# Foreign blocks of matmuls inside the next weight unit, five expert units per routing head, and two reordered row norms

## The chip, the cores and the metric

The kernel runs on one core of a Trainium2 chip. The metric is the device time of one execution in microseconds (us), the median of three runs. Engines are named as in the profile: PE is the matrix engine and PEld its weight loads, DVE the vector engine, ACT the scalar engine, POOL the general engine, SP the queue that issues most DMAs.

## What is computed

Two transformer-like blocks run one after the other over 16 meta tokens and 256 tokens of width 1024. The parts that the change touches, cut from the reference:

```python
# first block, after a gated convolution mixer (w_in, w_out):
q = (xf @ w_q).reshape(n_tok, 8, 256)                  # 8 routing heads
s1 = einsum("thd,hnd->thn", q[..., :128], sub_keys[:, 0]) # scores against 128 keys, twice
s2 = einsum("thd,hnd->thn", q[..., 128:], sub_keys[:, 1])
# top 16 of s1 and of s2, top 16 of their sums -> idx (of 16384 experts), gates = softmax
act = gelu(einsum("chkd,cd->chk", u[idx], xc))
out = einsum("chk,chkd->cd", act * gates, v[idx])      # 128 experts per token
# second block: rms norm, two attentions (8 heads each), sigmoid gates, then
hn = rmsnorm(h, norm_ffn_g)
h = h + (silu(hn @ w_ffn_gate) * (hn @ w_ffn_up)) @ w_ffn_down   # 2816 = 22 x 128
```

The experts are not gathered: the kernel computes all 16384 dense products with u, multiplies them by a gate matrix that is zero but for the chosen experts, and multiplies by all of v.

## The kernel before

**Units.** All weights are read as 453 units of 128x1024 numbers in one fixed list. For each unit SP loads `raw` (five buffers), ACT rounds it to `hi` and DVE computes `lo`, the rest (three buffers each). `unit()` hands out the next one and splits two ahead. A product is made of three matmuls, hi by hi, hi by lo and lo by hi.

**mm_w and mm_a.** `mm_w` makes one 128-row piece of a projection: 24 matmuls of 256 or 272 columns (eight chunks, three products) into one PSUM bank. `mm_a` accumulates a 1024-wide product over units into four banks: 12 matmuls of 512 columns per unit. The projections u (128 units of experts), q (two units per routing head), fg and fu (22 of each, the last block's gate and up projections) go through `mm_w`; v (128), wo, o and fd (22, the down projection) through `mm_a`.

**Order.** PE and SP run in the order in which the program is written. On ACT, DVE and POOL a scheduler sets the order when the program is built.

**Routing and gates.** The stage with u interleaves two other chains with the units. `route(hd)` makes the scores of a head (tile sc, four fp32 matmuls of 128 columns), then the top-16 searches on DVE. After the last head come `softmax`, `decode` and `flip`, and then `gates`, which for 64 groups of four tokens builds two one-hot factors on DVE (tiles ga, gb), multiplies them on PE (tile gp, four fp32 matmuls) and multiplies the result into the stored products on DVE and ACT (tiles ewa, ewb). A table of costs doles these chains out: after each unit `pull` runs as many of their steps as its credit allows. In the first stage a head takes two q units and `ROUTE` u units; when all heads have been started, u units go on until the chains are done, and then the rest of u runs with `gates`, until 126 units are done:

```python
    while todo:
        pull(10.0)
```

runs what is left of `gates` with no units between, then v begins with `expert_w(0)` (tiles w_hi, w_lo).

**Row norms.** In the first mixer and at the start of the second block the row scale is not applied to the input of a projection but to its result. `x_norm` (sum of squares by a matmul x_ss) and `across` (a diagonal matrix from the row scales, tile rsb_d, and two matmuls rsb_b or rsf_b) spread the scales over the partitions.

Of the kernel before, what the change touches and what calls it, by code (L numbers as in the profile page):

```python
# [1 line left out]

# [31 lines left out]
AHEAD = 400  # L34
XN = 1
SOON = 60
# [14 lines left out]
def two_blocks(ctx, tc, x, feats, vecs, w_in, w_out, w_q, keys, u, v, final_g, meta2, w_in2, lams, w_gate,  # L51
# [37 lines left out]
    units += [rows(w_out, c) for c in range(8)]  # L89
    ROUTE = 7  # L90
    nu = 0
# [70 lines left out]


    def mm_w(ps, a, cols):
        hi, lo = unit()
        ahi, alo = a
        for k in range(KC):
            ks = slice(k * P, (k + 1) * P)
            nc.tensor.matmul(ps, hi[:, ks], ahi[:, k, cols], start=(k == 0), stop=False)  # L169
            nc.tensor.matmul(ps, hi[:, ks], alo[:, k, cols], start=False, stop=False)  # L170
            nc.tensor.matmul(ps, lo[:, ks], ahi[:, k, cols], start=False, stop=(k == KC - 1))  # L171

    def mm_a(acc, parts, first, last):
        ws = [unit(1 if last else 2) for _ in parts]
        for t in range(2):
            ts = slice(t * P, (t + 1) * P)
            for n, ((ahi, alo), (hi, lo)) in enumerate(zip(parts, ws)):
                for b in range(2):
                    bs = slice(b * 512, (b + 1) * 512)
                    ps = acc[2 * t + b]  # L180
# [101 lines left out]
    for c in range(0, KC, 2):  # L282
        nc.sync.dma_start(xf[:, c:c + 2, :], feats[:, c:c + 2, :])
        if c < 4:
            load_part(c // 2)
    load_to(5)
# [4 lines left out]
    ident = const.tile([P, P], F32, tag="ident", name="ident")  # L291
    make_identity(nc, ident)


# [3 lines left out]
    for c in range(KC):  # L298
# [232 lines left out]

    def route(hd, qT, kt):
        yield None
        s = pr.tile([P, 2, 2, P], F32, tag="s", name=f"s{hd}", bufs=2)
        pss = mm_tile(f"sc{hd}")
        pv = pss.rearrange("p (t f n) -> p t f n", t=2, f=2)
        for t in range(2):
            for half in range(2):
                nc.tensor.matmul(pv[:, t, half, :], qT[half][:, t * P:(t + 1) * P], kt[:, half, :], start=True, stop=True)
        nc.scalar.activation(s, pv, AF.Copy)  # L540
        vv = pr.tile([P, 2, 2, TOPK], F32, tag="vv", name=f"vv{hd}", bufs=2)
        for t in range(2):
# [178 lines left out]
    for hd in range(NH):  # L721
# [3 lines left out]
        for half in range(2):  # L725
# [5 lines left out]
            pull(1.4)  # L731
        todo.append(route(hd, qT, kt))
        if hd == 3:
            todo.append(decode(0))
        if hd == NH - 1:
            todo.append(softmax())
            todo.append(decode(1))
            todo.append(flip())
        for j in range(ROUTE):
            expert_in(nu)  # L740
            nu += 1
            pull(1.5)
    while len(todo) > 0:
# [12 lines left out]
    later["s_g"].close()  # L756
    s_v, pv_ = phase("pv")
    wts = {}

    def expert_w(i):  # L760
# [8 lines left out]
        wts[i + 1] = hi2[:, 1, :], lo2[:, 1, :]  # L769

    expert_w(0)
    while nu < NK:
# [108 lines left out]

    def feat(name, hd, tag, cols, scale=1.0):
        width = cols.stop - cols.start
        ps = mm_tile(f"ps_{name}")
        mm_w(ps[:, :width], xT2, cols)
# [122 lines left out]
    for hd in range(NH):  # L1008
        q = feat(f"sq{hd}", hd, "sq", QS, float(P) ** -0.5)
        if hd > 0:  # L1010
            q = q()
            advance()
        k = feat(f"sk{hd}", hd, "k", FULL)
        if hd > 0:
# [73 lines left out]
    rsf = pf_.tile([P, T], F32, tag="rsf", name="rsf")  # L1088
    prev = []
    for m in range(NFF + 1):  # L1090
        if m < NFF:
            pg = mm_tile(f"fg{m}")
            mm_w(pg[:, :T], hT, slice(0, T))
            if m == 0:
                cols = [rms_rstd(pb, x2[t], P, f"r4_{t}", junk) for t in range(2)]
            pu = mm_tile(f"fu{m}")
            mm_w(pu[:, :T], hT, slice(0, T))
            if m == 0:
                across(pb, cols, rsf, "rsf")
                table(AF.Silu)  # L1100
            sl = pf_.tile([P, T], F32, tag="sl", name=f"sl{m}", bufs=2)
            nc.vector.tensor_tensor(sl, pg[:, :T], rsf, op=ALU.mult)
            sg = pf_.tile([P, T], F32, tag="sg", name=f"sg{m}", bufs=2)
            nc.scalar.activation(sg, sl, AF.Silu)
            nc.vector.tensor_tensor(sg, sg, rsf, op=ALU.mult)
            fa = pf_.tile([P, T], F32, tag="fa", name=f"fa{m}", bufs=2)
            nc.vector.tensor_tensor(fa, pu[:, :T], sg, op=ALU.mult)
            hi = pf_.tile([P, T], F32R, tag="f_hi", name=f"f_hi{m}", bufs=3)
            nc.scalar.activation(hi, fa, AF.Copy)
            lo = pf_.tile([P, T], F32R, tag="f_lo", name=f"f_lo{m}", bufs=3)  # L1110
            nc.vector.tensor_tensor(lo, fa, hi.bitcast(F32), op=ALU.subtract)
            prev.append((hi, lo))
        if 1 < m < NFF:
            mm_a(acc, [prev[m - 2]], m == 2, False)
        elif m == NFF:
# [84 lines left out]
```

## Time and profile before

| | |
|---|---|
| runs | 1470.22, 1470.78, 1472.76 us; median 1470.78 |
| profiled execution | 1472.7 us, of which the span (first to last instruction) is 1470.5 |
| busy share of the span | PE 98%, PEld 91%, DVE 72%, ACT 50%, POOL 1% |
| granted TensorE clock, mean | 0.993 of full speed |
| matmul records | 10096 |

A matmul's record lasts longer than the distance to the next one, since matmuls are pipelined: 284 ns on average for a u matmul. How fast PE goes is therefore read from the distance of starts, and the idle time from the waits. An fp32 matmul is recorded as two.

### The profile page before, as it was taken

The page shows a single profiled execution, that of the slowest core. Times are in us where ns is not written, and L with a number is a line of the kernel's source. Part 1 is how long each engine was busy: PE and PEld are TensorE (multiplying, and loading weights), DVE is VectorE, ACT ScalarE, POOL GpSimd, SP SyncE. Part 2 cuts the span into 40 slices and gives each one's busy share as a digit, 9 for nine tenths or more (in the row PEclk, how much of TensorE's full clock was granted, in tenths as well). Part 3 has the DMA queues.
Part 4 walks back from the last instruction along what each step waited for, and adds up shares of the span by engine and source line. Part 5 has one row for each costly group of instructions (what it writes and reads, how often), then busy time and mean ns, then how long its engine had stood idle before and what let it go on. Part 6 is the DMA issues. An engine that isn't in the chain of part 4 may idle for free.

```text
span 1470.5 us, 25555 instructions
## 1 busy us (share of the span) xinstructions
PE 1440.7 (98%) x10096; PEld 1341.6 (91%) x10096; DVE 1052.5 (72%) x1888; ACT 737.6 (50%) x1216; POOL 14.7 (1%) x35
## 2 busy tenths in 40 slices
PE   8999999999999999899999999999999999999998
PEld 7988999999999999688888888799999999899997
DVE  8987669679788999655555555665577776766665
ACT  7555444445444444244444444554455674544444
POOL 0010000000000000000000000100000000000000
PEclk9999999999999999999999999999999999999999
DMA  7525665665544444366666676553444455566562
GB/s 235 201 73 186 194 190 175 204 189 169 176 144 144 143 138 138 106 194 198 191 193 193 198 245 192 180 160 127 129 129 130 129 172 187 167 190 189 186 188 99
DMA packets 69815, 248.95 MB, mean 169 GB/s; under 512 B 7744, under 2 KB 9152, under 8 KB 69696
## 3 DMA queue, kind: packets, MB, share of 16 engines
q1 hardware_dynamic: 68544, 243.13, 52.6%
q0 software_dynamic: 1152, 4.19, 0.8%
q8 instruction: 79, 1.29, 0.4%
q14 instruction: 40, 0.33, 0.1%
HBM read 245.20 MB, written 2.10 MB: 168 GB/s over the span
## 4 chain that ended last, share of the span: by engine, by line
PE 94%; DVE 3%; DMA 1%; issue 1%; ACT 0%; SPq 0%; POOL 0%; DVEq 0%; ACTq 0%
PE u L171 8%; PE u L169 8%; PE u L170 8%; PE v L184 8%; PE v L183 8%; PE v L182 8%; PE gp L675 4%; PE fg L170 1%; PE fu L171 1%; PE fg L171 1%; PE fd L184 1%; PE fu L170 1%; PE fu L169 1%; PE fg L169 1%; PE fd L183 1%; PE fd L182 1%
## 5 line engine op out<-in xcount | busy, mean ns | idle before, releaser
L152 DVE TENSOR_TENSOR lo<-raw,hi 128x1024 fp32r<-128x1024 f32 x453 | 553.6, 1224 | 243.6 <-ACT hi L150 241.9
L150 ACT ACTIVATE hi<-raw 128x1024 fp32r<-128x1024 f32 x453 | 479.0, 1059 | 467.6 <-PE u L170 123.7
L169 PE MATMUL u<-hThi,hi 128*128 128x256 f32 x1024 | 290.5, 284 | 0.0
L171 PE MATMUL u<-hThi,lo 128*128 128x256 f32 x1024 | 285.7, 279 | 0.1
L170 PE MATMUL u<-hTlo,hi 128*128 128x256 f32 x1024 | 285.5, 279 | 0.0
L182 PE MATMUL v<-hi,w_hi 128*128 128x512 f32 x512 | 200.5, 392 | 1.3 <-ACT w_hi L764 1.3
L184 PE MATMUL v<-hi,w_lo 128*128 128x512 f32 x512 | 200.6, 392 | 0.5 <-DVE w_lo L766 0.5
L183 PE MATMUL v<-lo,w_hi 128*128 128x512 f32 x512 | 200.3, 391 | 0.1
L170 PEld LDWEIGHTS u<-hTlo,hi 128*128 128x128 f32 x1024 | 194.7, 190 | 0.0
L171 PEld LDWEIGHTS u<-hThi,lo 128*128 128x128 f32 x1024 | 192.2, 188 | 0.3 <-DVE lo L152 0.3
L169 PEld LDWEIGHTS u<-hThi,hi 128*128 128x128 f32 x1024 | 192.5, 188 | 0.0
L182 PEld LDWEIGHTS v<-hi,w_hi 128*128 128x128 f32 x512 | 96.8, 189 | 21.6 <-ACT w_hi L764 1.5
L184 PEld LDWEIGHTS v<-hi,w_lo 128*128 128x128 f32 x512 | 96.8, 189 | 21.3 <-DVE w_lo L766 1.0
L183 PEld LDWEIGHTS v<-lo,w_hi 128*128 128x128 f32 x512 | 96.8, 189 | 20.5 <-DVE lo L152 0.5
L675 PE MATMUL gp<-ga,gb 128*128 128x128 f32 x512 | 66.6, 275 | 4.0 <-DVE gb L666 4.0
L764 ACT ACTIVATE w_hi<-ewa 128x512 fp32r<-128x512 f32 x48 | 30.3, 633 | 77.4 <-PE v L183 66.7
L675 PEld LDWEIGHTS gp<-ga,gb 128*128 128x128 f32 x512 | 61.7, 191 | 4.8 <-PE gp L675 3.6
L766 DVE TENSOR_TENSOR w_lo<-ewa,w_hi 128x512 fp32r<-128x512 f32 x48 | 33.2, 693 | 39.4 <-ACT w_hi L764 39.4
L662 DVE TENSOR_TENSOR ga<-o,o 128x512 f32<-128x512 f32 x64 | 44.1, 689 | 17.7 <-PE gp L675 17.3
L170 PE MATMUL fg<-hTlo,hi 128*128 128x256 f32 x176 | 49.2, 279 | 0.5 <-DVE hTlo L223 0.5
L169 PE MATMUL fg<-hThi,hi 128*128 128x256 f32 x176 | 49.3, 280 | 0.3 <-ACT hThi L222 0.3
L171 PE MATMUL fu<-hThi,lo 128*128 128x256 f32 x176 | 49.1, 279 | 0.0
(407 smaller groups left out, 2957.3 us busy)
## 6 DMA issues: line engine op xcount, KB each, us to landing
raw<-in_u_dram SPq DMA_DIRECT2D x128, 512.0 KB, 3.6
raw<-in_v_dram SPq DMA_DIRECT2D x128, 512.0 KB, 3.6
raw<-in_w_in_dram SPq DMA_DIRECT2D x67, 512.0 KB, 3.6
raw<-in_w_fg_dram SPq DMA_DIRECT2D x22, 512.0 KB, 3.5
raw<-in_w_fu_dram SPq DMA_DIRECT2D x22, 512.0 KB, 3.5
raw<-in_w_fd_dram SPq DMA_DIRECT2D x22, 512.0 KB, 3.5
raw<-in_w_out_dram SPq DMA_DIRECT2D x16, 512.0 KB, 3.5
raw<-in_w_q_dram SPq DMA_DIRECT2D x16, 512.0 KB, 4.2
```

The costliest lines, as they stand in the source:

```text
L150: latest["hi"] = nc.scalar.activation(hi, loaded[i], AF.Copy)
L152: latest["lo"] = nc.vector.tensor_tensor(lo, loaded[i], hi.bitcast(F32), op=ALU.subtract)
L169: nc.tensor.matmul(ps, hi[:, ks], ahi[:, k, cols], start=(k == 0), stop=False)
L170: nc.tensor.matmul(ps, hi[:, ks], alo[:, k, cols], start=False, stop=False)
L171: nc.tensor.matmul(ps, lo[:, ks], ahi[:, k, cols], start=False, stop=(k == KC - 1))
L182: nc.tensor.matmul(ps, ahi[:, ts], hi[:, bs], start=first and n == 0, stop=False)
L183: nc.tensor.matmul(ps, ahi[:, ts], lo[:, bs], start=False, stop=False)
L184: nc.tensor.matmul(ps, alo[:, ts], hi[:, bs], start=False, stop=end)
L662: nc.vector.tensor_tensor(a.rearrange("p t (h l) -> p t h l", h=8), o8[:, tl, :].unsqueeze(3).broadcast_to((P, 4, 8, TOPK)), o16[:, tl, :] ...
L675: nc.tensor.matmul(p3[:, :, i], b[:, i, :], a[:, i, :], start=True, stop=True)
L764: nc.scalar.activation(hi, a, AF.Copy)
L766: nc.vector.tensor_tensor(lo, a, hi.bitcast(F32), op=ALU.subtract)
```

## The change

Five things are changed together.

- **A list of pending pieces.** `mm_w` runs what is in `pend` inside its own 24 matmuls: half of it after the 12th and the rest after the 15th. The scores of a head, the four gate products of a group, and in the last block the 12 fd matmuls of a unit are put there in two halves each, where before they stood as one block between units. `gates` empties the list itself at the start of each group.
- **Five u units** per routing head instead of seven (`ROUTE`), and a head's scores come in the first of them instead of after the second.
- **The first norm.** The first unit is loaded from ACT's queue ahead of all else, nine fp32 matmuls of ones by ones are put on PE ahead of the first product (`WARM`), the squares come after the split of the next unit, and x_ss after the second unit.
- **The norms of the second block.** The first q projection of head 1 is moved ahead of rsb_b; in the last block rsf_b and the first SwiGLU come one unit later.
- **mm_a** goes over the two units of its last call inside a bank, and not over the banks inside a unit.

The core of the diff:

```diff
-XN = 1
+XN = 2
+WARM = 9
...
-    ROUTE = 7
+    ROUTE = 5
...
-        nc.sync.dma_start(loaded[0][:, hs], units[0][:, hs])
+        nc.scalar.dma_start(loaded[0][:, hs], units[0][:, hs])
...
+    pend = []
+    def flush(n=None):
+        for f in pend[:n]:
+            f()
+        del pend[:n]
...
     def mm_w(ps, a, cols):
         hi, lo = unit()
         ahi, alo = a
         for k in range(KC):
+            if k == KC // 2:
+                flush((len(pend) + 1) // 2)
+            elif k == KC // 2 + 1:
+                flush()
...
-    def mm_a(acc, parts, first, last):
+    def mm_a(acc, parts, first, last, late=False):
         ws = [unit(1 if last else 2) for _ in parts]
-        for t in range(2):
+        def tokens(t):
             ts = slice(t * P, (t + 1) * P)
-            for n, ((ahi, alo), (hi, lo)) in enumerate(zip(parts, ws)):
-                for b in range(2):
+            for b in range(2):
+                for n, ((ahi, alo), (hi, lo)) in enumerate(zip(parts, ws)):
...
+        if late:
+            pend.extend(partial(tokens, t) for t in range(2))
+        else:
+            flush()
+            tokens(0)
+            tokens(1)
...
+    load_part(0)
+    load_part(1)
     nc.scalar.preload_act_table(AF.Sqrt)
...
+    for _ in range(WARM):
+        nc.tensor.matmul(warm[:, :P], ones, ones, start=True, stop=True)
...
-        if c % 2:
-            nc.scalar.activation(sq[:, c - 1:c + 1, :], xf[:, c - 1:c + 1, :], AF.Square)
+    split_to(2)
+    for c in range(0, KC, 2):
+        nc.scalar.activation(sq[:, c:c + 2, :], xf[:, c:c + 2, :], AF.Square)
...
+    def scores(hd, qT, kt):
...
+        pend.extend(partial(tokens, t) for t in range(2))
+        return pv
...
         for g in range(NG + 2):
+            flush()
...
-                for i in range(4):
-                    nc.tensor.matmul(p3[:, :, i], b[:, i, :], a[:, i, :], start=True, stop=True)
+                def pair(i0, a=a, b=b, p3=p3):
+                    for i in (i0, i0 + 1):
+                        nc.tensor.matmul(p3[:, :, i], b[:, i, :], a[:, i, :], start=True, stop=True)
                 banks[g - 1] = p3
+                pend.extend((partial(pair, 0), partial(pair, 2)))
...
-        todo.append(route(hd, qT, kt))
...
+        pv = scores(hd, qT, kt)
         for j in range(ROUTE):
             expert_in(nu)
             nu += 1
+            if j == 0:
+                todo.append(route(hd, pv))
...
-        q = feat(f"sq{hd}", hd, "sq", QS, float(P) ** -0.5)
-        if hd > 0:
+        q = feat(f"sq{hd}", hd, "sq", QS, float(P) ** -0.5) if hd != 1 else ahead
+        if hd > 1:
...
         if hd == 0:
+            ahead = feat("sq1", 1, "sq", QS, float(P) ** -0.5)
             with first():
                 across(pb, cols, rsb[:, QS], "rsb")
...
-            mm_a(acc, [prev[m - 2]], m == 2, False)
+            mm_a(acc, [prev[m - 2]], m == 2, False, late=True)
```

**Where instructions go.** On PE, at the end of the stage with u (u_7282 is the last unit of before, gp the gate products, v the first product with v), the program had:

```order
L171 MATMUL u_7282<-hThi,lo_7193 128x256
L675 MATMUL gp_7317<-ga_7231,gb_7233 128x128 x4
L675 MATMUL gp_7328<-ga_7278,gb_7280 128x128 x4
...
L675 MATMUL gp_7379<-ga_7368,gb_7370 128x128 x4
L182 MATMUL v_7396<-hi_7238,w_hi_7392 128x512
L183 MATMUL v_7396<-lo_7240,w_hi_7392 128x512
```

and has now, with u_7272 the 125th, u_7322 the 126th and u_7398 the 128th and last unit:

```order
L712 MATMUL gp_7268<-ga_7217,gb_7219 128x128 x2
L183 MATMUL u_7272<-hThi,hi_7177 128x256
L184 MATMUL u_7272<-hTlo,hi_7177 128x256
L185 MATMUL u_7272<-hThi,lo_7179 128x256
L712 MATMUL gp_7268<-ga_7217,gb_7219 128x128 x2
...
L712 MATMUL gp_7311<-ga_7264,gb_7266 128x128 x4
L183 MATMUL u_7322<-hThi,hi_7224 128x256
...
L185 MATMUL u_7398<-hThi,lo_7327 128x256
L197 MATMUL v_7432<-hi_7367,w_hi_7360 128x512
```

Before, seven groups of gp stood behind the last unit. Now the last group stands behind the 125th unit; the first one moved from behind the 75th to behind the 68th. Of the 64 groups 15 stand split inside a unit, as gp_7268, and 49 whole between units.

On PE at the start of the second block (ps_sq, ps_sk, ps_svT are the projections of a head, z the first attention product), the program had:

```order
L171 MATMUL ps_svT_10157<-xT2hi,lo_10070 128x272
L231 MATMUL rsb_b<-rsb_d_10189,ones 128x128
L231 MATMUL rsb_b<-rsb_d_10192,ones 128x128
L169 MATMUL ps_sq_10205<-xT2hi,hi_10099 128x256
...
L909 MATMUL z_10238<-sq_10197,kpad_10049 128x256
```

and has now:

```order
L183 MATMUL ps_sq_10224<-xT2hi,hi_10135 128x256
...
L253 MATMUL rsb_b<-rsb_d_10256,ones 128x128
L253 MATMUL rsb_b<-rsb_d_10259,ones 128x128
L183 MATMUL ps_sk_10272<-xT2hi,hi_10196 128x272
...
L952 MATMUL z_10305<-sq_10264,kpad_10085 128x256
```

The 24 matmuls of ps_sq moved from behind the second rsb_b to ahead of the first one; z keeps one projection, now ps_sk, between itself and rsb_b.

On ACT at the very start (xThi is the rounded input, hi_121 or hi_131 the first unit, sq the squares), the program had:

```order
L277 ACT_TABLE_LOAD
L300 ACTIVATE xThi<-xf,vec 128x272 x2
L142 ACTIVATE hi_121<-raw_90 128x512
L306 ACTIVATE sq<-xf 128x544
...
L306 ACTIVATE sq<-xf 128x544
L150 ACTIVATE hi_160<-raw_96 128x1024
L150 ACTIVATE hi_164<-raw_98 128x1024
```

and has now:

```order
L137 DMA raw_83<-in_w_in_dram 128x512 x2
L301 ACT_TABLE_LOAD
L144 ACTIVATE hi_131<-raw_83 128x512
L325 ACTIVATE xThi<-xf,vec 128x272 x4
L144 ACTIVATE hi_131<-raw_83 128x512
L325 ACTIVATE xThi<-xf,vec 128x272 x4
L152 ACTIVATE hi_149<-raw_96 128x1024
L332 ACTIVATE sq<-xf 128x544 x4
L152 ACTIVATE hi_174<-raw_98 128x1024
```

The four squares moved from between the roundings of the input to behind the rounding of the second unit, and the first half of the first unit stands ahead of the input.

## Rows read from the trace of the kernel before

**Rows 1.** The page, part 1: span, busy time by engine.

```profile
span 1470.5 us, 25555 instructions
PE 1440.7 (98%) x10096; PEld 1341.6 (91%) x10096; DVE 1052.5 (72%) x1888; ACT 737.6 (50%) x1216; POOL 14.7 (1%) x35
```

**Rows 2.** Waits of PE: engine, line, releaser; us in total, times, longest.

```profile
PE gg L169 <- ACT hi L142: 6.0, 1, 6.0
PE gp L675 <- DVE gb L666: 4.0, 5, 1.1
PE rsb_b L231 <- DVE rsb_d L230: 2.5, 1, 2.5
```

**Rows 3.** Stretches: us, busy PE, PEld, DVE, ACT, POOL (records), granted clock, DMA.

```profile
480.00:580.00 100.00, 100.00 (x874) 100.00 (x874) 93.21 (x177) 43.53 (x110) 0.00 (x0) 1.00 0.46 142
587.00:600.00 13.00, 7.66 (x58) 6.66 (x58) 12.90 (x29) 2.21 (x5) 0.00 (x0) 1.00 0.14 42
600.00:606.00 6.00, 5.49 (x14) 3.97 (x15) 1.69 (x3) 0.53 (x2) 0.00 (x0) 0.54 0.31 87
965.00:973.00 8.00, 5.55 (x32) 5.33 (x31) 3.95 (x15) 3.43 (x6) 0.00 (x0) 0.79 0.61 193
```

**Rows 4.** PE in order of time at the end of u: start, us, instruction, count.

```profile
586.93 1.95 PE L675 MATMUL gp<-ga,gb 128*128 128x128 f32 x16
...
599.87 0.50 PE L182 MATMUL v<-hi,w_hi 128*128 128x512 f32 x1 [1.31 <-ACT w_hi L764]
...
609.11 0.39 PE L182 MATMUL v<-hi,w_hi 128*128 128x512 f32 x1
...
611.83 0.39 PE L182 MATMUL v<-hi,w_hi 128*128 128x512 f32 x1
```

**Rows 5.** PE in order of time around rsb_b, second block.

```profile
965.06 0.38 PE L231 MATMUL rsb_b<-rsb_d,ones 128*128 128x128 f32 x2
967.89 0.49 PE L231 MATMUL rsb_b<-rsb_d,ones 128*128 128x128 f32 x2 [2.45 <-DVE rsb_d L230]
968.14 0.37 PE L169 MATMUL ps_sq<-xT2hi,hi 128*128 128x256 f32 x1
...
972.59 0.60 PE L909 MATMUL z<-sq,kpad 128*128 128x256 f32 x2
```

**Rows 6.** ACT and PE in order of time, the first 18 us.

```profile
4.46 0.94 ACT L300 ACTIVATE xThi<-xf,vec 128x272 fp32r<-128x272 f32 x2 [2.38 <-DMA xf<-in_feats_dram]
5.30 0.61 ACT L142 ACTIVATE hi<-raw 128x512 fp32r<-128x512 f32 x1
5.82 0.64 ACT L306 ACTIVATE sq<-xf 128x544 f32<-128x544 f32 x1
...
14.53 0.39 PE L171 MATMUL ga<-xThi,lo 128*128 128x272 f32 x1 [0.17 <-DVE lo L152]
...
17.66 0.28 PE L171 MATMUL gg<-xThi,lo 128*128 128x272 f32 x1
```

**Rows 7.** Stretches without gate products, the u instructions alone: us, busy PE (records), PEld, ACT.

```profile
166.00:178.00 12.00, 12.00 (x108) 12.00 (x108) 1.46 (x4) 1.00 0.55 175
327.00:379.00 52.00, 52.00 (x444) 52.00 (x443) 6.59 (x18) 1.00 0.59 188
```

**Rows 8.** ACT and DVE in order of time in the last block: the split of one unit.

```profile
1349.20 1.06 ACT L150 ACTIVATE hi<-raw 128x1024 fp32r<-128x1024 f32 x1 [1.55 <-issue]
...
1350.29 1.23 DVE L152 TENSOR_TENSOR lo<-raw,hi 128x1024 fp32r<-128x1024 f32 x1 [1.36 <-ACT hi L150]
```

**Rows 9.** PE in order of time around the scores of one head.

```profile
305.30 1.06 PE L539 MATMUL sc<-kt,qT 128*128 128x128 f32 x8
306.11 0.37 PE L169 MATMUL u<-hThi,hi 128*128 128x256 f32 x1
306.31 0.28 PE L170 MATMUL u<-hTlo,hi 128*128 128x256 f32 x1
```

More of the change, by code (lines that the diff above doesn't have):

```diff
@@ L1 @@
 from contextlib import ExitStack
+from functools import partial
 import concourse.bass as bass
@@ L171, in mm_w @@
             nc.tensor.matmul(ps, lo[:, ks], ahi[:, k, cols], start=False, stop=(k == KC - 1))
[L173 removed]
+    def mm_a(acc, parts, first, last, late=False):
         ws = [unit(1 if last else 2) for _ in parts]
[L175 removed]
+        def tokens(t):
             ts = slice(t * P, (t + 1) * P)
[L177 to L180 removed]
+            for b in range(2):
+                bs = slice(b * 512, (b + 1) * 512)
+                ps = acc[2 * t + b]
+                for n, ((ahi, alo), (hi, lo)) in enumerate(zip(parts, ws)):
                     end = last and n == len(parts) - 1
@@ L283, in two_blocks @@
         nc.sync.dma_start(xf[:, c:c + 2, :], feats[:, c:c + 2, :])
-        if c < 4:
-            load_part(c // 2)
     load_to(5)
@@ L292, in two_blocks @@
     make_identity(nc, ident)
+    warm = at_tile("warm")
+    for _ in range(WARM):
+        nc.tensor.matmul(warm[:, :P], ones, ones, start=True, stop=True)
     xT = (pc.tile([P, KC, L], F32R, tag="xThi", name="xThi"), pc.tile([P, KC, L], F32R, tag="xTlo", name="xTlo"))
@@ L529, in top16, with tokens, route, route_steps @@
         yield 3 * cost
-    def route(hd, qT, kt):
-        yield None
-        s = pr.tile([P, 2, 2, P], F32, tag="s", name=f"s{hd}", bufs=2)
+    def scores(hd, qT, kt):
         pss = mm_tile(f"sc{hd}")
         pv = pss.rearrange("p (t f n) -> p t f n", t=2, f=2)
-        for t in range(2):
+        def tokens(t):
             for half in range(2):
                 nc.tensor.matmul(pv[:, t, half, :], qT[half][:, t * P:(t + 1) * P], kt[:, half, :], start=True, stop=True)
+        pend.extend(partial(tokens, t) for t in range(2))
+        return pv
+    def route(hd, pv):
+        s = pr.tile([P, 2, 2, P], F32, tag="s", name=f"s{hd}", bufs=2)
         nc.scalar.activation(s, pv, AF.Copy)
+        return route_steps(hd, s)
+    def route_steps(hd, s):
         vv = pr.tile([P, 2, 2, TOPK], F32, tag="vv", name=f"vv{hd}", bufs=2)
@@ L741, in two_blocks @@
             nu += 1
+            if j == 0:
+                todo.append(route(hd, pv))
+                if hd == 3:
+                    todo.append(decode(0))
+                if hd == NH - 1:
+                    todo.append(softmax())
+                    todo.append(decode(1))
+                    todo.append(flip())
             pull(1.5)
@@ L757, in two_blocks @@
     s_v, pv_ = phase("pv")
+    later["pg"] = pv_
     wts = {}
@@ L769, in expert_w @@
         wts[i + 1] = hi2[:, 1, :], lo2[:, 1, :]
+    assert not pend
     expert_w(0)
@@ L880, in two_blocks, with feat @@
             nc.gpsimd.memset(o[:, n:], 0.0)
-    def feat(name, hd, tag, cols, scale=1.0):
+    def feat(name, hd, tag, cols, scale=1.0, spare=False):
         width = cols.stop - cols.start
-        ps = mm_tile(f"ps_{name}")
+        ps = (at_tile if spare else mm_tile)(f"ps_{name}")
         mm_w(ps[:, :width], xT2, cols)
@@ L1008, in two_blocks @@
     for hd in range(NH):
-        q = feat(f"sq{hd}", hd, "sq", QS, float(P) ** -0.5)
-        if hd > 0:
+        q = feat(f"sq{hd}", hd, "sq", QS, float(P) ** -0.5) if hd != 1 else ahead
+        if hd > 1:
             q = q()
             advance()
-        k = feat(f"sk{hd}", hd, "k", FULL)
+        k = feat(f"sk{hd}", hd, "k", FULL, spare=(hd == 1))
+        if hd == 1:
+            q = q()
+            advance()
         if hd > 0:
@@ L1089, in two_blocks, with swish @@
     prev = []
+    def swish(m, pg, pu):
+        sl = pf_.tile([P, T], F32, tag="sl", name=f"sl{m}", bufs=2)
+        nc.vector.tensor_tensor(sl, pg[:, :T], rsf, op=ALU.mult)
+        sg = pf_.tile([P, T], F32, tag="sg", name=f"sg{m}", bufs=2)
+        nc.scalar.activation(sg, sl, AF.Silu)
+        nc.vector.tensor_tensor(sg, sg, rsf, op=ALU.mult)
+        fa = pf_.tile([P, T], F32, tag="fa", name=f"fa{m}", bufs=2)
+        nc.vector.tensor_tensor(fa, pu[:, :T], sg, op=ALU.mult)
+        hi = pf_.tile([P, T], F32R, tag="f_hi", name=f"f_hi{m}", bufs=3)
+        nc.scalar.activation(hi, fa, AF.Copy)
+        lo = pf_.tile([P, T], F32R, tag="f_lo", name=f"f_lo{m}", bufs=3)
+        nc.vector.tensor_tensor(lo, fa, hi.bitcast(F32), op=ALU.subtract)
+        prev.append((hi, lo))
     for m in range(NFF + 1):
@@ L1095, in two_blocks @@
                 cols = [rms_rstd(pb, x2[t], P, f"r4_{t}", junk) for t in range(2)]
+            if m == 1:
+                across(pb, cols, rsf, "rsf")
+                table(AF.Silu)
+                swish(0, *first_two)
             pu = mm_tile(f"fu{m}")
@@ L1098, in two_blocks @@
             if m == 0:
[L1099 to L1112, printed above, removed]
+                first_two = pg, pu
+            else:
+                swish(m, pg, pu)
         if 1 < m < NFF:
-            mm_a(acc, [prev[m - 2]], m == 2, False)
+            mm_a(acc, [prev[m - 2]], m == 2, False, late=True)
         elif m == NFF:
```

6 lines of the change are left out of this document (removed).

## The prediction

> **What bounds the kernel now.** I read the busy times first: PE is busy for 1440.7 of 1470.5 us, 98% [rows 1]. Nothing else comes near, so only two things can shorten the time: PE's idle 29.8 us, and the pace of the matmuls. Next I read what PE waits for [rows 2]: 6.0 for the first rounded weights, 4.0 (five times) for the gate factors gb, 2.5 once for a diagonal rsb_d. Then I read the stretches around these waits, because a wait leaves a second cost: after the gate tail and around rsb_b the granted clock is 0.54 and 0.79, where it is 1.00 in the middle of the u stage [rows 3]. So a wait that goes takes its slow stretch along. Last I read PE's pace by the distance of starts.
>
> **The gate tail.** From the first of the last seven groups of gp to the first v matmul there are 599.87 − 586.93 = 12.94 us [rows 4]. The work in it is 56 records. What one takes is bounded by the gp rows (16 in 1.95, which includes the last one's drain, .122 [rows 4]) and the sc rows (8 in .81, .101 [rows 9]); I take .112, so 56 × .112 = 6.27. The other 6.67 is idleness: DVE is busy for 12.90 of the 13.00 and sets the pace [rows 3]. Then 24 v matmuls take 609.11 − 599.87 = 9.24. At full clock 12 take 611.83 − 609.11 = 2.72, .227 each, so 24 would take 5.45: 3.78 are lost to the low clock and a short wait [rows 4]. After the change no group stands behind the last unit. Three units lie between the last gp and v, 3 × 24 × .115 = 8.3 us of PE work, which covers the split of the first v units that PE waited for 1.31 us before [rows 4]. If both losses go, that is −6.67 − 3.78 = −10.45; if only the idleness goes and the clock is low all the same, −6.7.
>
> The seven groups must now be made earlier, under u units. DVE has little room there: between 480 and 580 it is busy for 93.21 of 100 us while PE never waits [rows 3]. They have seven more units for it, since the first gp now stands behind the 68th unit and not the 75th. The room is there, then, but thin: 6.8 us of DVE in 100. I add **+0.5** for new short waits on lo or gb, with the bounds 0 and +7 (the whole DVE deficit comes back). The earlier start also makes DVE fuller while the heads' searches run; PE waited nowhere there.
>
> **rsb_b.** PE waits 2.45 us for the second rsb_d, and the ps_sq behind it takes 972.59 − 968.14 = 4.45 us [rows 5] at a granted clock of 0.79 [rows 3]. Its 24 matmuls at .118, the slower of two paces below, are 2.84, so 1.6 more are lost. With ps_sq moved ahead it fills 965.06 to 967.90, and the second rsb_d was there for a start at 967.89 [rows 5]: the cover is just long enough. The wait and the clock loss go: **−4.05** (bounds −2.4, with only the wait gone, and −4.1). z still has one projection between rsb_b and itself, as before. If rsb_d comes later by as much as ps_sq shifts ACT and DVE, some tenths come back.
>
> **The start.** Before, ACT begins with the input at 4.46, rounds a first half unit at 5.30 (.61), and puts four squares of .64 between the rest [rows 6]; the first product waits until 6.0 [rows 2], and the third matmul of the second unit comes at 14.53, of the third unit at 17.66 [rows 6]. By hand now: the first unit is loaded ahead of the input, which I let land .4 later, at 4.9; the half unit can be rounded first, so the first product starts after one xThi (.47), at about 5.4. Then come seven more xThi (.47 each) and the other half (.61), which wait for the input's later pieces until about 9.7 as before, and ACT rounds the second unit (1.06 [rows 8]) to about 10.8; lo (1.23 [rows 8]) ends at 12.0 and not 14.53. The four squares (2.6) and the next unit (1.06) end at 14.4, its lo at 15.7 and not 17.66. I take the later point: **−2.0** (bounds −.8 and −3.0). The nine constant products are 18 records, 2.0 us at .112 and 4.0 at half clock; they end by about 5.1, before the first product can start, and cost nothing. If they don't raise the clock, a unit of 24 at half clock costs 24 × .118 = 2.8 and the gain is gone.
>
> The trace has xThi waiting 2.38 us for the input [rows 6], so loads are what starts the chain. The Trainium skill ("Trainium Kernel Development and Optimization", Key Constraints) says that DMAs issued from SP, ACT and POOL run on the same 16 engines and interleave, so that several issuers save only the issue time. By that the transfer of the first unit takes its bytes from the input's, and the gain would be nearer the lower bound, −.8; the −2.0 leans on ACT's order and not on faster loads.
>
> **The split blocks.** Fifteen gp groups, eight sc and twenty fd blocks, 43 in all, now stand in two halves inside a unit. The work is the same. Around an undivided sc block there is nothing to win or lose: eight records in .81, and .20 to the second u matmul behind it [rows 9]. I count **0**. The bounds are +8.6, if each of the 43 added halves brings a gap of .2 as between these two u matmuls, and −4.3, if each block had .1 of entry that overlaps now; I stay at 0, since eight records in .81 leave room for neither.
>
> **fd and rsf_b one unit later: 0.** fd's buffers are held for half a unit longer. By hand, for a round that begins with fg at 0: fd's second half ends at 4.5 (12 fg matmuls 1.4, 6 fd 1.4, 3 fg .3, 6 fd 1.4), fg at 5.5 and fu at 8.25. ACT rounds a unit in 1.06 and DVE takes 1.23 [rows 8], so the next fg's lo, after fd's, is ready at about 8.05, against 8.5 where its third matmul wants it: .45 to spare. Were that cover gone, 20 rounds would pay for each tenth 2 us. The inner order of mm_a's last call changes neither count nor cover: 0.
>
> **Two paces.** u matmuls run at two distances, at the same granted clock 1.00 [rows 7]: 444 records in 52.00 us, less two that reach over the edges, are 117.6 ns, and 108 in 12.00, less two, are 113.2. I find no cause; the pace changes where a foreign block or a short stall stands. u, q, fg and fu together are 128 + 16 + 44 units of 24 matmuls = 4512, and 4.4 ns on each is 19.9 us. Before it was about half and half, so the change, by shifting where the blocks stand, can move the time by up to ±9.9. I count 0, and it makes the range.
>
> **The sum.** −10.45 + .5 − 4.05 − 2.0 = −16.0. On the profiled execution's 1472.7 that is 1456.7; on the runs' median, 1.9 lower, 1454.8. I take **1454.8 us**, with 1451 to 1460 if the pace mix stays.
>
> **Rivals.** *The pace settles on the fast one* in most units: −16 − 9 gives about 1446. For it: halves inside a unit leave no block at a unit's border; against: no row says which place gives which pace. *The pace settles on the slow one*: about 1464. *The gate gain comes back as waits:* DVE, at 93 of 100, can't make 64 groups by the 125th unit without PE waiting; the 6.7 return as waits on lo or gb inside u and with them low clocks: about 1463. For it speaks DVE's share, against it that it had 6.8 us of room in each 100 and seven more units. *Little happens:* new waits in the q rounds and the last block eat the sum, 1468 to 1473.
>
> *Slower:* the halves make PE pause and its clock drops. One unit at half clock costs 2.8 us, so six of the 43 split units would undo the 16 us, and seven make it slower, about 1475. Against it: between 480 and 580 PE changes bank between u units and gp blocks all the time, at a granted clock of 1.00 [rows 3]. The Trainium skill ("TensorE: Matmul & The Clock Gate", "A second HAM failure mode: psum-queue depth-cycling") tells of a kernel that cycled through PSUM banks and paused so often between groups that its clock went up and down; a half block inside a unit is one more such change, and by that rule the time would rise to this rival's. The rows of 480 to 580 don't agree.
>
> **Numbers.** Likeliest .66 (1454.8); fast pace .12; slow pace .08; gate waits .08; little happens .03; slower .03. The range 1445 to 1464 takes in the first and the gate waits, and about half of the two paces: a little over 8 in 10. A measurement here tells .2%, 2.9 us, from no change: faster .94, same .03, slower .03.
>
> **What would show it.** At the end of u no wait on gb and a granted clock near 1.00 into v; rsb_b without a wait and ps_sq at .118; the first gg at about 5.4 and the third matmul of the third unit near 15.7; no wait of fg on lo in the last block; the distance of u starts still between 113 and 118 ns on average. I am wrong if PE waits on lo during the gates, if the clock falls inside split units, or if the sum holds while the pace of u moves.

## The result, and the profile after

The changed kernel takes 1456.02 us (median of four runs, 1455.48 to 1458.83) against 1470.5 for the kernel before on the same runs: a ratio of 0.9907, with a 95% interval from 0.9884 to 0.9931. The prediction was 1454.8. The profiled execution is the slowest of the four, 1458.83, with a span of 1456.8; it is 13.7 us below the span of before, and the terms below are read from these two spans.

The page's first part, answering to [rows 1]:

```profile
span 1456.8 us, 25628 instructions
PE 1437.5 (99%) x10114; PEld 1339.5 (92%) x10114; DVE 1049.4 (72%) x1887; ACT 741.1 (51%) x1236; POOL 14.5 (1%) x35
```

PE's waits, answering to [rows 2] (engine, line, releaser; us in total, times, longest):

```profile
PE gg L183 <- ACT xThi L325: 0.8, 1, 0.8
PE x_ss L341 <- DVE sq L259: 0.7, 1, 0.7
PE ga L185 <- DVE lo L154: 0.7, 1, 0.7
PE u L185 <- DVE lo L154: 0.6, 2, 0.3
PE q L185 <- DVE lo L154: 0.5, 2, 0.4
```

The waits of gp on gb, of rsb_b on rsb_d and of v on w_hi are gone. New is a wait of u and q on lo. It looks small here, and a view by stretches shows more of it, answering to [rows 3] (us; busy PE, PEld, DVE, ACT, POOL with records; granted clock; DMA share; GB/s):

```profile
3.00:6.00 3.00, 2.33 (x11) 2.03 (x10) 0.85 (x2) 1.10 (x4) 0.00 (x0) 1.00 0.99 361
140.00:200.00 60.00, 60.00 (x531) 60.00 (x530) 46.37 (x176) 29.73 (x45) 0.00 (x0) 1.00 0.61 192
212.00:260.00 48.00, 46.66 (x397) 45.47 (x397) 46.53 (x143) 22.65 (x35) 0.00 (x0) 1.00 0.63 190
480.00:580.00 100.00, 100.00 (x874) 100.00 (x873) 94.00 (x177) 43.80 (x110) 0.00 (x0) 1.00 0.46 143
585.00:600.00 15.00, 15.00 (x95) 13.54 (x94) 9.73 (x14) 8.15 (x14) 0.00 (x0) 1.00 0.60 176
944.00:950.00 6.00, 6.00 (x39) 6.00 (x39) 4.58 (x6) 3.02 (x6) 0.00 (x0) 0.72 0.70 233
1300.00:1400.00 100.00, 100.00 (x712) 93.64 (x711) 59.89 (x83) 44.35 (x59) 0.00 (x0) 1.00 0.58 185
```

Between 212 and 260, when the heads are searched, DVE is busy for 46.53 of 48 us and PE starts only 397 records where the row above has 531 in 60, which would be 425 in 48. The kernel before has more records of PE there, and less work on DVE:

```profile
212.00:260.00 48.00, 47.85 (x415) 47.43 (x415) 42.95 (x94) 22.80 (x35) 0.00 (x0) 1.00 0.59 183
```

From 585 to 600 the handover from u to v now runs at full clock. At 944 there is a new stretch at .72, one unit behind tr_x; it is spoken of below. The row of 3 to 6 us belongs to the start, and the rows at 140 and 1300 to the pace, which is the distance between the starts of two matmuls of 256 columns.

PE in order of time where u ends and v begins, answering to [rows 4]:

```profile
591.39 0.28 PE L185 MATMUL u<-hThi,lo 128*128 128x256 f32 x1
591.51 0.40 PE L197 MATMUL v<-hi,w_hi 128*128 128x512 f32 x1
...
596.97 0.39 PE L197 MATMUL v<-hi,w_hi 128*128 128x512 f32 x1
```

The first 24 v matmuls take 596.97 − 591.51 = 5.46, where they took 9.24 [rows 4]. And around rsb_b, answering to [rows 5]:

```profile
956.86 0.28 PE L185 MATMUL ps_sq<-xT2hi,lo 128*128 128x256 f32 x1
956.98 0.60 PE L253 MATMUL rsb_b<-rsb_d,ones 128*128 128x128 f32 x4
957.34 0.37 PE L183 MATMUL ps_sk<-xT2hi,hi 128*128 128x272 f32 x1
```

Both rsb_b stand in one row without a wait, and the unit behind follows .36 later. The start, answering to [rows 6], on ACT, DVE and PE:

```profile
5.54 0.94 ACT L325 ACTIVATE xThi<-xf,vec 128x272 fp32r<-128x272 f32 x2 [0.83 <-DMA xf<-in_feats_dram]
...
6.11 0.39 PE L183 MATMUL gg<-xThi,hi 128*128 128x272 f32 x1 [0.79 <-ACT xThi L325]
...
12.15 0.40 PE L185 MATMUL ga<-xThi,lo 128*128 128x272 f32 x1 [0.72 <-DVE lo L154]
...
14.31 1.22 DVE L154 TENSOR_TENSOR lo<-raw,hi 128x1024 fp32r<-128x1024 f32 x1
15.45 0.43 DVE L259 TENSOR_TENSOR sq<-sq 128x272 f32<-128x272 f32 x1
15.94 0.73 PE L341 MATMUL x_ss<-sq,ones 128*128 128x272 f32 x2 [0.74 <-DVE sq L259]
16.30 0.49 PE L183 MATMUL gg<-xThi,hi 128*128 128x272 f32 x1
...
16.75 0.28 PE L185 MATMUL gg<-xThi,lo 128*128 128x272 f32 x1
```

The input arrives 1.08 later than before, the first product starts .14 later, and the third matmul of the third unit stands at 16.75 and not at 17.66. Its lo is ready at 15.53 (14.31 + 1.22); x_ss stands ahead of it on PE and waits for DVE's sum of the squares.

### The profile page after: what moved, and what is told of

Its sections match the earlier page's. It is cut to its first block, busy times and chain, and to the rows that moved or that the text cites. A ratio compares the mean times of both kernels' runs of the same rounds, so it can differ in the third digit from the quotient of the medians.

```text
span 1456.8 us, 25628 instructions
## 1 busy us (share of the span) xinstructions
PE 1437.5 (99%) x10114; PEld 1339.5 (92%) x10114; DVE 1049.4 (72%) x1887; ACT 741.1 (51%) x1236; POOL 14.5 (1%) x35
## 4 chain that ended last, share of the span: by engine, by line
PE 92%; DVE 6%; issue 1%; ACT 0%; DMA 0%; SPq 0%; DVEq 0%; ACTq 0%
PE v L197 8%; PE v L199 8%; PE v L198 8%; PE u L185 7%; PE u L183 7%; PE u L184 7%; PE gp L712 4%; DVE lo L154 2%; PE fg L184 1%; PE fg L185 1%; PE fu L185 1%; PE fu L183 1%; PE fu L184 1%; PE fg L183 1%; PE fd L199 1%; PE fd L198 1%
## 5 line engine op out<-in xcount | busy, mean ns | idle before, releaser
L712 PE MATMUL gp<-ga,gb 128*128 128x128 f32 x512 | 69.9, 274 | 0.0
L183 PE MATMUL fu<-hThi,hi 128*128 128x256 f32 x176 | 49.6, 282 | 0.0
```

## The experiments

After the traces were compared, three theories were on the table. **Theory 1**: the gain is the gate tail and rsb_b, less waits that five units per head bring; and an undivided foreign block flips the pace of the matmuls behind it between 113 and 118 ns (F, fast, and S, slow, below), while two halves three matmuls apart flip it and flip it back. The rival to this second part is that the pace belongs to a place or a stage. **Theory 2**, that only blocks over a length flip it, and **theory 3**, that transposes set the fast pace, came up for the ladder, e9.

"Before" is the kernel before, timed again beside each run.

| run | median, us (runs) | ratio to before, interval |
|---|---|---|
| e1, seven units per head | 1463.51 (10) | 0.9961, 0.9949 to 0.9974 |
| e2, blocks undivided | 1457.22 (4) | 0.9918, 0.9894 to 0.9943 |
| e3, first fd block undivided | 1459.72 (4) | 0.9932, 0.9908 to 0.9956 |
| e4, ps_sq not ahead | 1456.90 (5) | 0.9917, 0.9889 to 0.9944 |
| e5, late flush | 1456.16 (4) | 0.9905, 0.9876 to 0.9934 |
| e6, no constant products | 1457.55 (4) | 0.9923, 0.9894 to 0.9952 |
| e7, old start | 1455.36 (4) | 0.9907, 0.9875 to 0.9940 |
| e8, six units per head | 1456.09 (4) | 0.9911, 0.9883 to 0.9940 |
| e9, ladder | 1470.29 (1) | one run |
| e10, transposes ahead | 1460.94 (5) | 0.9942, 0.9929 to 0.9954 |
| e11, the same, six units | 1462.25 (5) | 0.9953, 0.9940 to 0.9966 |
| e12, changed kernel again | 1453.62 (6) | 0.9901, 0.9886 to 0.9915 |

The changed kernel's ten runs lie between 1450.98 and 1458.83, so medians a microsecond or two apart say little, and most of what follows is read from single stretches of the traces.

**e1: seven units per head.**

```diff
-    ROUTE = 5
+    ROUTE = 7
```

> The changed kernel with seven u units per head again; all else as changed. Theory 1 (the gate tail went because the gates start seven units earlier): at least six gp groups stand behind the last unit again, DVE paces them, and v starts at half clock. +6.7 and +3.8 come back, and the short waits on lo that the changed kernel has in the head stage (some 3 us) go: about 1463.5 us. Rival (the split or the new order took the tail away): within 2 us of the changed kernel's 1456.0.

Measured 1463.51, +7.5. Its waits and two stretches around the end of u:

```profile
PE gp L712 <- DVE gb L701: 3.3, 4, 1.1
...
PE v L197 <- ACT w_hi L806: 1.3, 1, 1.3
```

```profile
586.00:599.00 13.00, 8.39 (x67) 7.56 (x65) 12.67 (x28) 2.26 (x6) 0.00 (x0) 1.00 0.20 75
599.00:605.00 6.00, 5.46 (x16) 4.07 (x17) 1.80 (x3) 1.00 (x2) 0.00 (x0) 0.72 0.29 90
```

Six groups stand behind the last unit, DVE is busy for 12.67 of 13 us, and v begins at a clock of .72. The tail is 5.7 us of idleness by the distance of starts, v loses 2.6, and u and q no longer wait on lo in the heads. The splitting is untouched here, so the tail went by the five units, as theory 1 says.

**e2: every block undivided**, at the place of its first half, behind the 12th matmul.

```diff
             if k == KC // 2:
-                flush((len(pend) + 1) // 2)
-            elif k == KC // 2 + 1:
                 flush()
```

> The changed kernel with every foreign block undivided, at the place of the first half (behind the 12th matmul of a unit). Theory 1 (an undivided foreign block flips the pace of the matmuls behind it between 113 and 118 ns; two halves three matmuls apart flip it and flip it back): the heads' u and q units alternate again, so slow ones rise from 872 of 3360 to about half (+3.5 us), and the last block alternates in place of 118 throughout (-2.1): about 1457.5 us, with fast fg and fu matmuls near half. Rival (the pace hangs on the place inside the unit or on the stage): fg and fu stay at 118, the heads at 113, and the time within 1 us of 1456.0. Second rival (halves cost an entry each): about 2 us less throughout, in each stretch with halves.

**e5: halves for nearly all gate groups.**

```diff
         for g in range(NG + 2):
-            flush()
...
                 yield 1.4
+            flush()
             if 0 <= g - 1 < NG:
```

> The changed kernel with the pending gate products emptied in the middle of a group's step and not at its start, so that 55 of 64 groups stand in halves inside a unit and 9 undivided (changed: 15 and 49). Theory 1: the u matmuls of the gate stage, which alternate between 113 and 118 ns with each undivided group, keep the pace of the unit before for most of the 57 units: if that is 113, up to 28 x 24 x 4.4 ns = -3 us, about 1453; if it is 118, +3. Rival: pace by place or stage, no change, 1456. Should DVE get its products too late, waits on gb or ab appear and the time rises.

**e12: the changed kernel again.**

> The changed kernel itself, to have it on the same chip and to see the last block again. Theory 1 (the pace at the start of the last block is chance, and the halves keep it to the end): fg to the last fd takes 183.0 or 187.0, nothing between; the time 1452 to 1460, median 1456. Rival (the 187.0 belongs to this program): 187.0 again.

These three belong together. The number of PE records in a stretch of the heads and in one of the last block, at a granted clock of 1.00; e2 first, then e5, then e12, with two more stretches of e12:

```profile
140.00:200.00 60.00, 60.00 (x523) 60.00 (x523) 45.64 (x171) 29.75 (x45) 0.00 (x0) 1.00 0.61 190
1300.00:1400.00 100.00, 100.00 (x720) 93.53 (x719) 59.97 (x84) 46.70 (x60) 0.00 (x0) 1.00 0.63 190
```

```profile
140.00:200.00 60.00, 60.00 (x513) 60.00 (x513) 44.24 (x161) 28.41 (x43) 0.00 (x0) 1.00 0.61 189
1300.00:1400.00 100.00, 100.00 (x730) 93.59 (x729) 62.02 (x86) 45.67 (x60) 0.00 (x0) 1.00 0.61 190
```

```profile
140.00:200.00 60.00, 60.00 (x531) 60.00 (x530) 46.37 (x176) 29.73 (x45) 0.00 (x0) 1.00 0.63 192
280.00:340.00 60.00, 60.00 (x512) 60.00 (x511) 48.33 (x96) 31.32 (x47) 0.00 (x0) 1.00 0.57 184
1262.00:1270.00 8.00, 7.03 (x41) 6.40 (x42) 5.92 (x11) 5.06 (x9) 0.00 (x0) 0.79 0.30 91
1300.00:1400.00 100.00, 100.00 (x730) 93.64 (x729) 61.59 (x86) 46.36 (x62) 0.00 (x0) 1.00 0.60 192
```

With halves such a stretch is all fast (531, 730) or all slow (512 or 513, 712 in the changed kernel's first trace), in any combination, and the code of the last block is the same in each; in e12 the heads turn from fast to slow at a stall on lo at 248 us. Undivided, both stretches lie in the middle (523, 720): slow distances of u and q rise from 872 to 1760 of some 3370, and half of fg and fu run fast, as theory 1 expected of e2. From the first to the last fd matmul the traces of kernels with all fd blocks in halves take 167.36 or 167.37 us four times (the changed kernel, e1, and e10 and e11 behind their added blocks) or 163.95 to 164.11 six times (e4 to e8, e12), and nothing between; e2 takes 165.56. From the first fg on, the measure named ahead of e12, e12 takes 184.82, which does lie between: its first fg unit ran at a low clock (.79 from 1262 to 1270), which cost 1.8. So the 118 ns of the first trace doesn't belong to the program, and the halves don't make the mean pace better: they hold the pace that happens to reach them. e5's bet was lost: its heads ran slow from their start, and so did most of the gate stage (907 of 1200 distances of u, 759 of 1282 in the changed kernel). From the first matmul of the 69th u unit to v e5 takes 225.46 against 223.61, of which eight more gp records make .9.

Over all fourteen traces, read from the distance of starts on both sides of each block: undivided blocks of sc (8 records), gp (8 or 16) and fd (12 matmuls) flipped the pace 711 times out of 711; two halves kept it 538 times out of 539.

**e3: the first fd block undivided.**

```diff
-            mm_a(acc, [prev[m - 2]], m == 2, False, late=True)
+            mm_a(acc, [prev[m - 2]], m == 2, False, late=(m > 2))
```

> The changed kernel with the first of the 20 fd blocks undivided, between units, and the other 19 in halves as they are. Theory 1 (an undivided block flips the pace, halves keep it): from that block on fg and fu run at 113 ns to the end: 1056 matmuls less some 110 ahead of it, 4.4 ns each, -4.1 us, about 1452. Rival (the last block runs at 118 for another reason): no change but for the place of one block, 1456.

Measured 1459.72. The block did flip the pace, but it had come in fast (all of the last few units ahead of it), so the other 19 rounds ran slow. The mechanism held, and the forecast of −4.1 was wrong by its sign: one flip helps only who knows the pace ahead of it.

**e4: ps_sq behind rsb_b again** (ahead, its place in the loop and the spare bank undone).

```diff
-        q = feat(f"sq{hd}", hd, "sq", QS, float(P) ** -0.5) if hd != 1 else ahead
-        if hd > 1:
+        q = feat(f"sq{hd}", hd, "sq", QS, float(P) ** -0.5)
+        if hd > 0:
...
-            ahead = feat("sq1", 1, "sq", QS, float(P) ** -0.5)
```

> The changed kernel with the first q projection of head 1 behind rsb_b again. Theory 1 (the step took away the wait and the slow clock behind it): the wait of 2.4 on rsb_d comes back, and a part of the slow clock; in the changed trace the stretch from the first tr_x to the first ps_dq is 2.8 shorter than before, so about +2.8, 1458.8 us. Rival (the wait moves elsewhere, or the clock loss at the first ps_sq, which grew by 1.6 in the changed trace, belongs to this step): +4.1 or +1.2, and the first ps_sq at the pace of before.

Its rsb_b, and the tile view's lines for the first tr_x and the first ps_dq (count, ns shortest, median, longest, and the time from first to last); then those of e12:

```profile
954.50 0.54 PE L253 MATMUL rsb_b<-rsb_d,ones 128*128 128x128 f32 x2 [2.33 <-DVE rsb_d L252]
...
L241 PE MATMUL tr_x<-ident,x x16: 272/273/303, 938.9 to 941.5; 128*128 128x128 f32 x16
...
L183 PE MATMUL ps_dq<-xT2hi,hi x64: 277/282/388, 1044.4 to 1132.8; 128*128 128x256 f32 x64
```

```profile
L241 PE MATMUL tr_x<-ident,x x16: 271/273/301, 942.4 to 945.0; 128*128 128x128 f32 x16
...
L183 PE MATMUL ps_dq<-xT2hi,hi x64: 277/283/387, 1043.6 to 1132.0; 128*128 128x256 f32 x64
```

The wait is back, and the stretch takes 1044.4 − 938.9 = 105.5 against 1043.6 − 942.4 = 101.2: the step is worth 4.3. The median, 1456.9, can't show that beside the two paces, which were both fast in e4's trace. The changed kernel's first trace takes 102.7 because its first ps_sq ran at .72 of the clock (944 to 950 above); the other traces of the changed order don't have that, so neither of the two expectations was right about this 1.5: it is no part of the step. Where that low clock comes from stays open.

**e6: no constant products, and e7: the old start.**

```diff
-WARM = 9
+WARM = 0
```

> The changed kernel without the nine constant products at the start. Theory 1 (they raise the clock ahead of the first product): the first unit runs at half clock, its 24 matmuls at .227 in place of .127 where they don't wait, up to 2.4 us; but the input arrives slowly, and the third matmul of the second unit waits for lo at 12.15 in any case, so about +1.0 and less than +2.4: 1457. Rival (the input's arrival sets the pace of the first unit whatever the clock): within .3 of 1456.0.

```diff
-WARM = 9
+WARM = 0
-XN = 2
+XN = 1
...
-        nc.scalar.dma_start(loaded[0][:, hs], units[0][:, hs])
+        nc.sync.dma_start(loaded[0][:, hs], units[0][:, hs])
...
-    split_to(2)
...
+        if c % 2:
+            nc.scalar.activation(sq[:, c - 1:c + 1, :], xf[:, c - 1:c + 1, :], AF.Square)
```

> The changed kernel with the whole start of before: the first unit loaded by SP between the input's pieces, no constant products, the squares between the roundings, x_ss behind the first unit. Theory 1: the changed trace is 1.0 ahead at the first cg unit, so +1.0 here and nothing later: 1457.0 us, and the first xThi at 4.5 in place of 5.5. Rival (the 2.0 of the prediction was there and something else lost 1.0 of it): +2.0.

In e6 the first unit runs at half pace (.23 a matmul) to its 14th matmul, and still the third matmul of the second unit is only .25 later than in the changed kernel, since lo is what it waits for:

```profile
6.06 0.60 PE L183 MATMUL gg<-xThi,hi 128*128 128x272 f32 x1 [6.06 <-ACT xThi L325]
...
12.40 0.39 PE L185 MATMUL ga<-xThi,lo 128*128 128x272 f32 x1 [0.72 <-DVE lo L154]
```

Even this .25 isn't the products': the last xThi ends at 10.14 in e6 and at 9.89 in the changed kernel, and in both the matmul shown stands 2.26 behind that end and the first unit of the projection cg 27.49 behind the matmul. That is e6's rival: the nine products are worth nothing here. e7 reaches the first cg unit at 40.44 us of the span, the changed kernel at 39.65, eight other traces of its start between 39.2 and 39.7, and two at 40.1 and 40.3: the whole new start is worth about 1.0. Both medians, 1457.55 and 1455.36, can't tell that.

**e8: six units per head.**

```diff
-    ROUTE = 5
+    ROUTE = 6
```

> The changed kernel with six u units per head. Theory 1 (five units make DVE the bound in the head stage, seven leave a tail): the waits of u and q on lo between 212 and 260 us, some 3 us with the slow matmuls behind them, go, and one or two gp groups stand behind the last unit, DVE-paced at 1.85 each with a low clock after: -3 and +2 to +5, so 1455 to 1458. Rival (the waits on lo come from the decode after head 3, whatever the number of units): the waits stay and the tail is added, 1459 to 1461.

Measured 1456.09. PE waits on lo in the heads for 3.1 us by the distance of starts (3.9 with five units, .9 before), two groups stand behind the last unit with 1.8 of idleness, and v loses .9. So the waits stay, as the rival has it, and a tail is added. The median lies where theory 1 put it all the same; the trace, with both stretches fast, shows one way to such a time.

**e9: a ladder of constant blocks** in the last block, one in each round.

```diff
+    LADDER = ("m1", "m2", "m3", "m4", "t2", "t3", "t6")
...
+        if 2 <= m < NFF:
+            block(LADDER[(m - 2) % 7], f"lad{m}")
```

> The changed kernel with one more block of constant fp32 products (128 columns) or transposes ahead of each of the rounds 2 to 21 of the last block, between a fu and a fg unit, in a repeating list of seven: 1, 2, 3 and 4 products (2, 4, 6 and 8 records), and 2, 3 and 6 transposes (as many records). Their results are not used. Each shows what such a block does to the pace, 113 or 118 ns, between the fu ahead of it and the first half of the fg behind it. Theory 1 (an undivided block flips the pace, whatever it is made of and however long): 20 flips in 20 rounds, time up by some 11 us for 130 more records at .111 less nothing: 1456 + 11. Theory 2 (only blocks over a length flip: rsf_b with 4 records mostly kept the pace, 8 always flipped it): flips behind 8 records alone. Theory 3 (transposes set the fast pace: 9 of 10 times behind the six of eT and gT): 113 behind every block of transposes, whatever was ahead.

The blocks came to 87 records, and not to the 130 of the expectation. What stood ahead of each block and behind it (F is 113 ns, S 118):

```
1 product  (2 records): F S, F S, F S      2 transposes: S F, F S, F S
2 products (4 records): S F, S S, S S      3 transposes: F F, S F, S F
3 products (6 records): F S, S F, S F      6 transposes: F F, F F
4 products (8 records): S S, F F, F F
```

One flip in the trace, PE in order of time:

```profile
1278.61 0.28 PE L184 MATMUL fu<-hTlo,hi 128*128 128x256 f32 x1
1278.72 0.28 PE L185 MATMUL fu<-hThi,lo 128*128 128x256 f32 x1
1278.84 0.38 PE L1158 MATMUL lad<-ones 128*128 128x128 f32 x2
1278.98 0.36 PE L183 MATMUL fg<-hThi,hi 128*128 128x256 f32 x1
```

One product is enough to flip, so theory 2 (length) falls; four of constants keep the pace, though four of gp always flip it, so theory 1 doesn't hold for every block either. Three and six transposes always left the fast pace here, which would be theory 3. Twelve of the twenty blocks flipped the pace.

**e10 and e11: three transposes to set the fast pace.**

```diff
+        if hd in (0, 3, 6):
+            set_fast(at_tile(f"set{hd}"))
         pv = scores(hd, qT, kt)
...
+        if m == 2:
+            set_fast(mm_tile("set_fd"))
```

> The changed kernel with three transposes of constants between the last q and the first u unit of heads 0, 3 and 6, and ahead of the first fd block: 12 records, 1.3 us. Theory 3 (three or more transposes set the fast pace, and the halves behind them keep it): the last block at 113 ns in every execution (fg to the last fd 183.0 + .3, against 187.0 or 183.0 by chance), most of the heads' units too. The mean over the two paces that the executions of the changed kernel show is about 1456; from it -2 in the last block, -2 in the heads (the waits on lo take half back), +1.3: about 1453.5, with less spread. Rival (the fast pace behind the transposes was chance): slow stretches behind some of the four, +1.3: about 1457.

> The same with six u units per head. With five, PE in the fast pace waits 3.9 us on lo in the heads; six gave 3.2 and 2.8 lost at the end of u (tail 1.9, low clock .9). Theory 1: no gain over five, 1453 to 1456. Rival (with the pace set, DVE's load per unit decides, and six take the waits away): 2 us below five.

Measured 1460.94 and 1462.25, against 1453.62 for e12 beside them. Theory 3 falls at once: in both kernels all eight blocks of three transposes flipped what was ahead, six of them from fast to slow. Both expectations of e10 missed its time. Its heads and last block, for the most part in the slow pace:

```profile
132.00:190.00 58.00, 58.00 (x496) 58.00 (x496) 44.96 (x173) 28.72 (x44) 0.00 (x0) 1.00 0.60 183
280.00:340.00 60.00, 60.00 (x512) 60.00 (x511) 48.83 (x103) 31.53 (x46) 0.00 (x0) 1.00 0.57 185
1300.00:1400.00 100.00, 100.00 (x712) 93.64 (x711) 61.23 (x84) 44.85 (x60) 0.00 (x0) 1.00 0.59 186
```

No version was found that beats the changed kernel by more than the spread of its own runs.

## Why the prediction was right, point by point

The time was 1.2 us above the forecast. The terms, read from the profiled executions of the changed kernel and of e12, which is the same program, against that of before:

| term | predicted | measured | e12 |
|---|---|---|---|
| gate tail, and v behind it | −10.45 | −6.7 − 3.8 = −10.5 | −10.5 |
| new waits of u and q | +.5 | +3.0 | +2.1 |
| rsb_b | −4.05 | −2.8 | −4.3 |
| start | −2.0 | −1.0 | −1.0 |
| pace, u and q | 0 | −4.0 | 0 |
| pace, last block | 0 | +2.1 | −1.9 + 1.8 (low clock) |
| end | 0 | −.6 | −.6 |
| sum | −16.0 | −13.8 (the spans: −13.7) | −14.4 (the spans: −14.8) |

That the number came out so near is in part luck. The terms that were worked out bring −11.3 in the first trace and not −16.0; the pace, which the sum had at 0, gives 1.9 back in this execution. By the prediction's own list it is wrong "if the sum holds while the pace of u moves", and that is what the first trace shows: slow distances of u and q (115.5 to 130 ns) fell from 1780 to 872 of some 3400. In e12 they are 1714, so this part of the gain isn't the change's.

- **The gate tail** went as worked out, the idleness and the slow clock both, and e1 shows that the five units per head did it. The .112 per gp record, an estimate there, is what the distances of starts give (.1116).
- **"I add +0.5 for new short waits on lo or gb"** is the step that was mis-sized. It looked for them in the gate stage, where DVE's share rose only from 93.21 to 94.00 of 100 and PE doesn't wait. They came where I had written that "PE waited nowhere there": with five u units for the same searches DVE is busy for 46.53 of 48 us in the heads (42.95 before), and u and q wait on lo for 3.9 us (the distances of starts over 130 ns behind the first q unit, less 115.5 each) against .9 before. So PE did wait there before, where the records of the matmuls, which overlap, hide most of it from the busy time (47.85 of 48). The rival on returning waits had the right mechanism at the wrong place, and about half of its price. Where an execution runs the heads in the slow pace these waits are smaller (1.3 in e5); that PE then asks for less per microsecond is the likely reason, which no run isolates.
- **rsb_b**: the term was right, and a little small: 4.3 by e4 and e12, where its bound was 4.1. The 1.5 by which the first trace misses it is a low clock behind tr_x that other traces of the same order don't show.
- **The start** is the second term that was mis-sized, by a step left out of the chain. The input landed 1.08 later and not .4 (5.54 against 4.46 [rows 6]), while the DMA share was .99 at 361 GB/s (3 to 6 us). All twelve traces that load the first unit ahead of the input begin their first xThi at 5.49 or later, before and e7 at 4.46 and 4.16: what is loaded first delays what comes behind. The rule of the Trainium skill ("Trainium Kernel Development and Optimization", Key Constraints) that the prediction had weighed, of queues that share the same DMA engines, agrees with this delay. The loss of 1.0 isn't in it, though: the last xThi ends at 9.89, the second unit's lo at 12.10 and the third's at 15.53, where the hand-made chain had 9.7, 12.0 and 15.7. What the chain lacked is x_ss, which the change itself puts on PE between the second and the third unit. It starts at 15.94, .74 late, behind DVE's sum of the squares, and the third matmul of the third unit follows at 16.75; in all twelve traces that matmul stands 1.21 to 1.23 behind the end of its lo. That the gain came near the bound of .8, which the prediction gave by that rule, is a coincidence.
- **The split blocks: 0.** They brought no pause and no drop of the clock: between 140 and 200 and between 1300 and 1400 PE is busy throughout, at a granted clock of 1.00. The rule of the Trainium skill ("TensorE: Matmul & The Clock Gate", "A second HAM failure mode: psum-queue depth-cycling") tells of a clock that suffers from frequent pauses between groups in different PSUM banks; here the bank changes brought no such pauses, so no run puts that rule to the test, and the rival on the slower side falls. What they do is what the prediction left open as "two paces": they keep the pace of an execution where undivided blocks alternate it. In the first trace that gave 4.0 in the heads and took 2.1 in the last block, where fg and fu had none fast; in e12 it gave nothing in the heads and 1.9 in the last block.
- **fd and rsf_b later: 0** was right. PE has no wait on lo in the last block, at 712 records in 100 us slow and 730 fast.
- **The end** gave .6 that I had at nothing: the last banks now come due one after the other, and DVE's multiplication of the third quarter by its gain (.69) runs ahead of the last bank's addition, where it stood behind it before.

## What to carry to other kernels

A rate change that moves a side chain earlier must be costed where the chain then runs: look at the busy share of its engine in that stretch, not in the stretch that it leaves. A chain worked out by hand must hold every instruction that stands ahead of its end in the engine's order, those too that the change moves there (here x_ss). When single executions of one program differ by half a percent, compare stretch by stretch and count records at the same clock before any median is explained. Where several edits come together, the ones that set a persistent state (here the pace) need the same program run again, because one trace shows only one of its values.

## What the runs showed of the hardware that was not expected

Matmuls of 256 columns against hThi and hTlo have two steady paces at a granted clock of 1.00: 531 against 513 records in 60 us of the heads, 730 against 712 in 100 us of the last block. A pace lasted until a block of other matmuls or a stall, but for one turn in e2 (at 301 us) with neither; an undivided sc, gp or fd block turned it every time (711 of 711), two halves with three matmuls between them returned it (538 of 539). Blocks of constants don't follow one rule by length: one product turned it three times in three, four products never in three, three transposes ten times in eleven. Which property of a block counts, and what the pace is made of, stays open, and no block was found that sets the fast one.
